# Layer 1's last group: another order for DVE's and ScalarE's steps behind the last convolution and in the closing ring

## The chip, the cores and the metric

The kernel runs on one core of one Trainium2 chip. The core has five engines that follow their own instruction lists and wait for one another on semaphores: TensorE (PE) multiplies matrices into PSUM banks, VectorE (DVE) and ScalarE (ACT) do elementwise work, GpSimd (POOL) does elementwise work and starts some transfers, and SyncE (SP) starts the others. The metric is the device time of one execution in microseconds (us), as the median of several runs.

## The reference

The computation is a two-layer decoder trunk on 512 tokens of 1024 channels, in float32. Layer 0 mixes tokens by causal pooling, layer 1 by sliding-window attention. Behind each mixer comes a gated MLP with a causal depthwise convolution of width 3, and at the end a final RMS norm:

```python
def rms_norm(x, g):
    xf = x.astype(jnp.float32)
    y = xf * lax.rsqrt(jnp.mean(xf * xf, axis=-1, keepdims=True) + RMS_EPS)
    return (y * g.astype(jnp.float32)).astype(x.dtype)

def conv_glu_ffn(h, w_in, conv_w, conv_b, w_out):
    u = h @ w_in
    c = conv(u, conv_w) + conv_b          # causal, depthwise, width 3
    a, g = c[..., :D_FF], c[..., D_FF:]
    return (a * jax.nn.silu(g)) @ w_out

def reference(x, ...):
    h = x
    for i in range(DEPTH):
        hn = rms_norm(h, norm_mix[i])
        ...
        h = h + mix
        hn = rms_norm(h, norm_ffn[i])
        h = h + conv_glu_ffn(hn, ffn_w_in[i], ffn_conv_w[i], ffn_conv_b[i], ffn_w_out[i])
    return rms_norm(h, norm_f)
```

`D_FF` is 2816. The change lies at the very end: in the last part of layer 1's `(a * silu(g)) @ w_out`, the residual add and the final norm.

## The kernel before

Every float32 product is made of three matmuls. Each operand is split into a high part, rounded by ScalarE (`A.activation(h, raw, AF.Copy)`, L105 for weights, L774 for activations), and a low part, the rest, which DVE subtracts (L108, L776). `mm3` issues high by high (L89), high by low or low by high (L90), and the third cross product (L91).

**Layer 1's MLP, first half** (`mlp_in`). The 2816 hidden channels are 22 blocks of 128, each with a gate half (s = 1) and a value half (s = 0). For each half TensorE fills a PSUM bank with the product over all 512 tokens. `conv_chunk` then makes the convolution of it: ScalarE scales the bank by the last tap (L689), DVE adds the two shifted taps (L690, L691). The gate goes through ScalarE's silu (L750), and DVE multiplies the halves (L761).

**Layer 1's MLP, second half** (`mlp_tokens`). Pairs of blocks and pairs of token halves are multiplied by Strassen's scheme with seven products instead of eight. For this DVE forms sums and differences of a block pair's activations (L765 to L767, tile `y`); `split_sum` splits them into `zh` and `zl` (L774, L776), seven slices of 256 tokens. The output weights come as blocks a11, a12, a22 and as sums s1 to s4, each split in the same way. The 11 pairs of blocks are worked in three groups of 4, 4 and 3 pairs (`GROUPS`); the change touches the last one, for which `end` is set. Its pairs come in a first set of two and a second set of one. The second set's pair is block pair 10, the last one, so its `zh` and `zl` come last of all. The steps of this group are a11 of both sets, s1, a12 and s2 of the first set, s1, a12 and s2 of the second, and then s4, s3 and a22 of both sets. Each step makes two banks (q = 0 and 1), one per token quarter of 128.

A step's banks are added into the residual tile `ht`, which holds tokens in rows. In the last group a11, s1 and s2 are subtracted at L905 in `evict`. The banks that complete half a quarter's row go to the class `Last`. `left` takes the first 512 channels of a token quarter (quarters 0 and 1 behind a12, 2 and 3 behind s4) and `right` the others (quarters 2 and 3 behind s3, 0 and 1 behind a22). Both call `gather`: DVE adds the bank (L957), ScalarE squares and sums the row (L959, tile `n_sq`, sums in `ss`). `gained` lets GpSimd multiply the left half by the norm's gain (L964, tile `hg`). The reciprocal root is made of tiny steps of one element a row: two scalings on DVE (L996, L997), a square root on ScalarE (L969, `rs_y`), then on DVE L970, a reciprocal (L971) and one Newton step (L976, L977) into `r`. `store` scales the two halves by `r`, the right one on DVE (L985) and the left one on ScalarE (L987), and sends both out (L989). This handing of a quarter from engine to engine is the ring. Before the first square, `gather` has ScalarE load its square-root table (L954, then L123), with an input from the last `zh`.

**What sets the order.** Most instructions are placed by the framework's scheduler, which lists each engine's instructions at build time. `tc.issue_after(x)` keeps an instruction behind `x`, and `pin` keeps the pinned instructions of an engine in program order. On the chip every engine works its list strictly in order. In the last group the scheduler may place all weight splits but three, and the subtractions of L905, only behind the last sum of the activations (`sums[-1]`, L767).

Two banks (76 and 77, `alpha`) are reused by a11, s2, s3 and a22 in turn, so TensorE's first matmul of s2 waits until DVE has subtracted a11's bank.

Of the kernel before, what the change touches and what calls it, by code (L numbers as in the profile page):

```python
# [23 lines left out]
ALU = mybir.AluOpType  # L24
# [3 lines left out]
D = 1024  # L28
# [9 lines left out]
NF = FF // P  # L38
# [24 lines left out]
def trunk(ctx: ExitStack, tc: tile.TileContext, x_tok, x_t, vecs, w_pool, w_kq, w_v, w_o, gain, w_in, w_half, w_down, w_tok, out):  # L63
# [630 lines left out]
    def mlp_in(fp, layer, xs, norm, z, turns):  # L694
# [25 lines left out]
        for i, group in enumerate(groups):  # L720
# [21 lines left out]
            for n, ((j, s), ps) in enumerate(zip(group, pss)):  # L742
                with ExitStack() as order:
                    for x in () if i else behind[: 3 + n // 2]:
                        order.enter_context(tc.issue_after(x.ins))
                    conv[s] = conv_chunk(fp, layer, ps, None if i else rb, s * NF + j, f"c{layer}_{j}_{s}")
                if i:
                    turn(3, *taps[-2:])
                if s == 1:
                    silu = A.activation(conv[1], conv[1], AF.Silu)  # L750
                    if i:
                        turn(1, silu, taps[-1])
                    continue
                e, odd = divmod(j, 2)
                if not odd:
                    y = fp.tile([P, 8, HS], F32, tag="y", name=f"y{layer}_{e}", bufs=1)
                    zh = fp.tile([P, 7, HS], F32R, tag="zh", name=f"zh{layer}_{e}", bufs=5)
                    zl = fp.tile([P, 7, HS], F32R, tag="zl", name=f"zl{layer}_{e}", bufs=5)
                    z.append((zh, zl))
                o = y[:, 2 * odd : 2 * odd + 2, :].rearrange("p a b -> p (a b)")  # L760
                V.tensor_tensor(o, conv[0], conv[1], ALU.mult)  # L761
                if not odd:
                    split_sum(y, z[e], 0, 0, 1, -1.0)
                else:
                    V.tensor_tensor(y[:, 4:6, :], y[:, 0:2, :], y[:, 1:4:2, :], ALU.subtract)  # L765
                    V.tensor_tensor(y[:, 6, :], y[:, 4, :], y[:, 3, :], ALU.add)
                    sums.append(V.tensor_tensor(y[:, 7, :], y[:, 2, :], y[:, 6, :], ALU.subtract))  # L767
                    split_sum(y, z[e], 2, 1, 6)
                yield j

# [9 lines left out]
    def mlp(fp, xs, norm):  # L780

        z, ht = [], []
        turns = turned(fp, ht)
        up = mlp_in(fp, 1, xs, norm, z, turns)
        done, first = 0, 0
        for g, n in enumerate(GROUPS):
            upto = first + 2 * n
            end = Last(fp, z, ht) if upto == NF else None
            while done < min(upto + 1, NF):
                done = next(up) + 1  # L790
                if end and done in (NF - 3, NF - 2):
                    end.split("a22" if done == NF - 3 else "a12", g)
            for x in turns:
                pass
            mlp_tokens(g, z[first // 2 : upto // 2], ht, end)
            first = upto

    def turned(fp, ht):
# [15 lines left out]
                    )  # L814
                    yield

    def mlp_tokens(g, z, ht, end):

        sets = [(sum(SETS[g][:i]), sum(SETS[g][: i + 1])) for i in range(len(SETS[g]))]
        raws, banks_of = {}, {}  # L820
# [44 lines left out]
        def ready(upto):  # L865
            while todo and len(ws) < upto + kept:
                x = todo.pop(0)
                with ExitStack() as order:
                    if end and x not in (("a11", 0), ("a11", 1), ("s1", 0)):
                        order.enter_context(tc.issue_after(sums[-1].ins))  # L870
                    ws[x] = split(*x)

# [33 lines left out]

        used = 0
        for kind, s in steps:
            ready(used + AHEAD + 1)
            used += not end or (kind, s) not in end.ws  # L910
            name = KINDS[kind][1]
# [16 lines left out]
    class Last:  # L928
        def __init__(self, fp, z, ht):
# [1 line left out]
            self.r = small(fp, NT, 32, name="r3", bufs=1)  # L931
            self.ss = small(fp, 2 * NT, 32, name="ss3", bufs=1)
            self.root_in = small(fp, 1, 32, name="root1_in", bufs=1)
            self.fp, self.ws = fp, {}

        def split(self, kind, g):
            whole = tuple(
# [28 lines left out]
        def root(self, t):  # L966
            v, e = self.mid[t]
            s1 = self.ss[:, 2 * t + 1 : 2 * t + 2]
            pin(A.activation(e, s1, AF.Sqrt, bias=e, scale=1.0 / D))  # L969
            pin(V.scalar_tensor_tensor(v, s1, -0.5 / D, v, ALU.mult, ALU.add))  # L970
            pin(V.reciprocal(e, e))  # L971

        def newton(self, t):
            v, e = self.mid[t]
            x = self.tiny("t")
            pin(V.scalar_tensor_tensor(x, e, e, v, ALU.mult, ALU.mult))  # L976
            pin(V.scalar_tensor_tensor(self.r[:, t : t + 1], x, 1.5, e, ALU.add, ALU.mult))  # L977

# [12 lines left out]
        def left(self, t, ps):  # L991
            self.gather(t, 0, ps)
            self.gained(t, 0)
            v, e = self.mid[t] = self.tiny("v"), self.tiny("y")
            s0 = self.ss[:, 2 * t : 2 * t + 1]
            pin(V.tensor_scalar(v, s0, -0.5 / D, -0.5 * EPS, ALU.mult, ALU.add))  # L996
            pin(V.tensor_scalar(e, s0, 1.0 / D, EPS, ALU.mult, ALU.add))  # L997

        def right(self, t, ps):
            last, was = t == 1, self.prev  # L1000
            if was is not None:
                self.root(was)
            self.gather(t, 1, ps)
            if was is not None:
                self.newton(was)
                if not last:
                    self.store(was)
            self.prev = t

        def close(self):  # L1010
            self.store(0, (1,))
            self.root(1)
            self.store(0, (0,))
            self.newton(1)
            self.store(1, eng=A)

    norm0, norm1, norm2 = (Norm(f"n{i}") for i in range(3))
    xs0, xs1, xs2 = [], [], []
# [354 lines left out]
```

## Time and profile before

| what | value |
|---|---|
| median of 3 runs | 892.71 us (892.08 to 893.31) |
| profiled execution, its own time | 892.47 us |
| span of the profiled execution | 890.4 us |
| granted TensorE clock | 0.997 |
| TensorE busy | 878.3 us, 99% of the span |
| DVE busy | 702.4 us, 79% |
| ScalarE busy | 509.3 us, 57% |
| GpSimd busy | 252.7 us, 28% |

The span runs from the first to the last instruction; the device time has 2.07 us more around it. In the rows of a timeline the columns are the start in the span, the duration, the engine, the line, the operation and its output and inputs with their shapes. At the end, in brackets, stands the idle time of the engine ahead of the instruction and what ended it. Consecutive instructions of one engine overlap a little, so the distance from start to start is what one costs its queue. The end of the kernel, from the last matmul of the convolution on, is the part from about 852 us to 890.4 us.

### The profile page before, as it was taken

How to read it: one execution, taken by the hardware profiler on the slowest of the kernel's cores; microseconds unless marked ns; L12 is line 12 of the kernel's file. 1: busy time of each engine (PE TensorE's matmuls, PEld its weight loads, DVE VectorE, ACT ScalarE, POOL GpSimd, SP SyncE). 2: the span in 40 equal slices, each digit the busy share in tenths (PEclk: the TensorE clock that was granted, in tenths of full speed). 3: DMA queues.
4: the chain of work that ended last, by engine and by line, in shares of the span. 5: the costliest groups of instructions: out<-in, count | busy, mean ns of one | idle time of the engine just before them, and what ended most of it. 6: DMA issues, size and time to landing. Idle time of an engine off the chain costs nothing.

```text
span 890.4 us, 12922 instructions
## 1 busy us (share of the span) xinstructions
PE 878.3 (99%) x4720; PEld 760.1 (85%) x4720; DVE 702.4 (79%) x1106; ACT 509.3 (57%) x851; POOL 252.7 (28%) x331
## 2 busy tenths in 40 slices
PE   8999999999999999999999999999999999999996
PEld 8888889999999998888888888888888888888875
DVE  6989998888788886765887386997876777866886
ACT  7856655646455553635888365887634444434544
POOL 4767332222213110335765040000330002200212
PEclk9999999999999999999999999999999999999998
DMA  8444346565555542222110042364486221572332
GB/s 323 143 138 119 110 135 180 148 172 148 145 155 155 127 144 81 73 95 95 49 48 25 1 144 93 112 170 144 89 209 199 95 95 48 136 231 83 119 71 95
DMA packets 38559, 109.98 MB, mean 124 GB/s; under 512 B 4064, under 2 KB 6112, under 8 KB 38496
## 3 DMA queue, kind: packets, MB, share of 16 engines
q1 hardware_dynamic: 34464, 95.26, 33.0%
q0 software_dynamic: 3888, 13.63, 9.0%
q8 instruction: 37, 0.61, 0.3%
q10 hardware_dynamic: 144, 0.26, 0.1%
q14 instruction: 26, 0.21, 0.1%
HBM read 107.04 MB, written 2.10 MB: 123 GB/s over the span
## 4 chain that ended last, share of the span: by engine, by line
PE 83%; DVE 12%; ACT 3%; issue 2%; DMA 1%; POOL 0%; ACTq 0%; DVEq 0%
PE bank L89 26%; PE bank L90 26%; PE bank L91 26%; PE bank L1208 1%; PE bank L1236 1%; DVE bank L395 1%; PE bank L290 1%; DVE tl L414 1%; PE bank L257 1%; ACT sc L1224 1%; DVE uw_hold_l L470 1%; DVE a_t L376 1%; DVE a_t L361 0%; DVE wt_a_l L108 0%; DMA wi_raw<-w_in 0%
## 5 line engine op out<-in xcount | busy, mean ns | idle before, releaser
L89 PE MATMUL bank<-f1x_h,wi_h 128*128 128x512 f32 x352 | 137.1, 389 | 0.0
L90 PE MATMUL bank<-f1x_l,wi_h 128*128 128x512 f32 x352 | 136.9, 389 | 0.0
L91 PE MATMUL bank<-f1x_h,wi_l 128*128 128x512 f32 x352 | 136.8, 389 | 0.0
L105 ACT ACTIVATE wi_h<-wi_raw 128x1024 fp32r<-128x1024 f32 x58 | 61.4, 1058 | 58.7 <-PE bank L90 38.3
L108 DVE TENSOR_TENSOR wi_l<-wi_raw,wi_h 128x1024 fp32r<-128x1024 f32 x44 | 53.8, 1222 | 37.0 <-ACT wi_h L105 36.9
L91 PEld LDWEIGHTS bank<-f1x_h,wi_l 128*128 128x128 f32 x352 | 66.1, 188 | 14.0 <-DVE wi_l L108 0.2
L89 PEld LDWEIGHTS bank<-f1x_h,wi_h 128*128 128x128 f32 x352 | 66.1, 188 | 13.7
L90 PEld LDWEIGHTS bank<-f1x_l,wi_h 128*128 128x128 f32 x352 | 66.1, 188 | 13.6
L487 POOL TENSOR_TENSOR uw_r_raw<-uw_r_raw,uw_u_raw 128x512 f32<-128x512 f32 x15 | 25.0, 1667 | 161.7 <-DVE uw_hold_l L470 148.9
L108 POOL TENSOR_TENSOR wi_l<-wi_raw,wi_h 128x256 fp32r<-128x256 f32 x56 | 53.1, 979 | 29.4 <-ACT wi_h L105 19.0
L842 POOL TENSOR_TENSOR wt_a_raw<-wt_a_raw,wt_s_raw 128x1024 f32<-128x1024 f32 (+1 forms) x6 | 13.9, 2322 | 144.4 <-DVE wt_a_l L108 141.8
L91 PE MATMUL bank<-th,uw_hold_l 128*128 128x256 f32 x180 | 50.9, 283 | 0.0
L90 PE MATMUL bank<-tl,uw_hold_h 128*128 128x256 f32 x180 | 50.9, 283 | 0.0
L89 PE MATMUL bank<-th,uw_hold_h 128*128 128x256 f32 x180 | 50.8, 282 | 0.0
L830 POOL DMA_DIRECT2D wt_s_raw<-w_tok x12 | 10.4, 869 | 141.0 <-DMA wt_s_raw<-w_tok 86.3
L222 POOL TENSOR_TENSOR n_acc<-n_acc,n_sq 128x512 f32<-128x512 f32 x13 | 19.1, 1468 | 86.6 <-ACT n_sq L213 86.5
L90 PE MATMUL bank<-f0x_l,wi_h 128*128 128x512 f32 x112 | 43.6, 389 | 0.0
L91 PE MATMUL bank<-f0x_h,wi_l 128*128 128x512 f32 x112 | 43.6, 389 | 0.0
L89 PE MATMUL bank<-f0x_h,wi_h 128*128 128x512 f32 x112 | 43.0, 390 | 0.0
L469 ACT ACTIVATE uw_hold_h<-wo_raw 128x512 fp32r<-128x512 f32 (+1 forms) x48 | 28.4, 591 | 25.4 <-PE bank L90 18.8
L533 DVE TENSOR_TENSOR h<-bank,h 128x512 f32<-128x512 f32 x48 | 32.9, 686 | 11.9 <-PE bank L91 11.4
L689 ACT ACTIVATE c_t<-bank,vec 128x512 f32<-128x512 f32 x44 | 33.4, 766 | 8.2 <-PE bank L91 5.2
(440 smaller groups left out, 2826.7 us busy)
## 6 DMA issues: line engine op xcount, KB each, us to landing
wi_raw<-w_in SPq DMA_DIRECT2D x58, 512.0 KB, 3.3
wo_raw<-w_down SPq DMA_DIRECT2D x32, 256.0 KB, 2.7
uw_u_raw<-w_half SPq DMA_DIRECT2D x15, 512.0 KB, 5.6
uw_u_raw<-w_half POOLq DMA_DIRECT2D x15, 512.0 KB, 5.7
uw_r_raw<-w_half SPq DMA_DIRECT2D x15, 512.0 KB, 3.5
wt_a_raw<-w_tok SPq DMA_DIRECT2D x15, 512.0 KB, 3.9
wt_s_raw<-w_tok SPq DMA_DIRECT2D x11, 512.0 KB, 3.9
kq_raw<-w_kq SPq DMA_DIRECT2D x10, 512.0 KB, 3.3
```

The lines of the kernel that those rows point to most:

```text
L89: T.matmul(ps, lhsT=wh, rhs=xh, start=start, stop=False, **kw)
L90: T.matmul(ps, lhsT=wh, rhs=xl, start=False, stop=False, **kw)
L91: T.matmul(ps, lhsT=wl, rhs=xh, start=False, stop=stop, **kw)
L105: pin(A.activation(h[:, :n], raw[:, :n], AF.Copy))
L108: lows.append((eng or V).tensor_tensor(l[:, o], raw[:, o], h[:, o].bitcast(F32), ALU.subtract))
L222: eng.tensor_tensor(self.acc[:, lo:hi], self.acc[:, lo:hi], sq[:, lo:hi], ALU.add)
L469: A.activation(w[0], raw, AF.Copy)
L487: G.tensor_tensor(r[:, :n], r[:, :n], u[:, n:], ALU.add)
L533: V.tensor_tensor(h[m], ps, h[m], ALU.add)
L689: taps.append(A.activation(t, ps, AF.Identity, bias=col(V_CB + layer * 2 * NF + m), scale=cw[2]))
L830: pin(G.dma_start(r[:, :n], src[:, b1, :], accum_op=ALU.add))
L842: G.tensor_tensor(r[:, :n], r[:, :n], raws["s1", s][:, :n], ALU.add)
```

## The change

The diff:

```diff
--- before.py
+++ after.py
@@ -765,6 +765,8 @@
                     V.tensor_tensor(y[:, 4:6, :], y[:, 0:2, :], y[:, 1:4:2, :], ALU.subtract)
                     V.tensor_tensor(y[:, 6, :], y[:, 4, :], y[:, 3, :], ALU.add)
                     sums.append(V.tensor_tensor(y[:, 7, :], y[:, 2, :], y[:, 6, :], ALU.subtract))
+                    if j == NF - 1:
+                        yield j
                     split_sum(y, z[e], 2, 1, 6)
                 yield j
 
@@ -792,7 +794,7 @@
                     end.split("a22" if done == NF - 3 else "a12", g)
             for x in turns:
                 pass
-            mlp_tokens(g, z[first // 2 : upto // 2], ht, end)
+            mlp_tokens(g, z[first // 2 : upto // 2], ht, end, up)
             first = upto
 
     def turned(fp, ht):
@@ -814,7 +816,7 @@
                     )
                     yield
 
-    def mlp_tokens(g, z, ht, end):
+    def mlp_tokens(g, z, ht, end, up):
 
         sets = [(sum(SETS[g][:i]), sum(SETS[g][: i + 1])) for i in range(len(SETS[g]))]
         raws, banks_of = {}, {}
@@ -867,6 +869,7 @@
                 x = todo.pop(0)
                 with ExitStack() as order:
                     if end and x not in (("a11", 0), ("a11", 1), ("s1", 0)):
+                        order.enter_context(tc.issue_after(taps[-2].ins))
                         order.enter_context(tc.issue_after(sums[-1].ins))
                     ws[x] = split(*x)
 
@@ -906,6 +909,8 @@
 
         used = 0
         for kind, s in steps:
+            if end and (kind, s) == ("a12", 0):
+                next(up)
             ready(used + AHEAD + 1)
             used += not end or (kind, s) not in end.ws
             name = KINDS[kind][1]
@@ -931,7 +936,7 @@
             self.r = small(fp, NT, 32, name="r3", bufs=1)
             self.ss = small(fp, 2 * NT, 32, name="ss3", bufs=1)
             self.root_in = small(fp, 1, 32, name="root1_in", bufs=1)
-            self.fp, self.ws = fp, {}
+            self.fp, self.ws, self.due = fp, {}, []
 
         def split(self, kind, g):
             whole = tuple(
@@ -967,12 +972,13 @@
             v, e = self.mid[t]
             s1 = self.ss[:, 2 * t + 1 : 2 * t + 2]
             pin(A.activation(e, s1, AF.Sqrt, bias=e, scale=1.0 / D))
-            pin(V.scalar_tensor_tensor(v, s1, -0.5 / D, v, ALU.mult, ALU.add))
-            pin(V.reciprocal(e, e))
 
         def newton(self, t):
             v, e = self.mid[t]
             x = self.tiny("t")
+            s1 = self.ss[:, 2 * t + 1 : 2 * t + 2]
+            pin(V.scalar_tensor_tensor(v, s1, -0.5 / D, v, ALU.mult, ALU.add))
+            pin(V.reciprocal(e, e))
             pin(V.scalar_tensor_tensor(x, e, e, v, ALU.mult, ALU.mult))
             pin(V.scalar_tensor_tensor(self.r[:, t : t + 1], x, 1.5, e, ALU.add, ALU.mult))
 
@@ -991,28 +997,31 @@
         def left(self, t, ps):
             self.gather(t, 0, ps)
             self.gained(t, 0)
+            self.halves()
+            self.due.append(t)
+
+        def halves(self):
+            while self.due:
+                self.half(self.due.pop())
+
+        def half(self, t):
             v, e = self.mid[t] = self.tiny("v"), self.tiny("y")
             s0 = self.ss[:, 2 * t : 2 * t + 1]
             pin(V.tensor_scalar(v, s0, -0.5 / D, -0.5 * EPS, ALU.mult, ALU.add))
             pin(V.tensor_scalar(e, s0, 1.0 / D, EPS, ALU.mult, ALU.add))
 
         def right(self, t, ps):
-            last, was = t == 1, self.prev
-            if was is not None:
-                self.root(was)
+            was, self.prev = self.prev, t
             self.gather(t, 1, ps)
+            self.halves()
+            self.root(t)
             if was is not None:
                 self.newton(was)
-                if not last:
-                    self.store(was)
-            self.prev = t
+                self.store(was, (1, 0))
 
         def close(self):
-            self.store(0, (1,))
-            self.root(1)
-            self.store(0, (0,))
-            self.newton(1)
-            self.store(1, eng=A)
+            self.newton(self.prev)
+            self.store(self.prev, eng=A)
 
     norm0, norm1, norm2 = (Norm(f"n{i}") for i in range(3))
     xs0, xs1, xs2 = [], [], []
```

It has three parts. First, the generator `mlp_in` stops ahead of the last `split_sum` and is resumed by `mlp_tokens` ahead of a12's first step; `ready` also keeps most weight splits behind the second last tap (`taps[-2]`, ScalarE's first step of the last convolution). On DVE the steps behind the last convolution then stand in another order. In these lists `y` is the tile of the last block pair's sums, `wt_0` and `wt_1` are the weights of the first and second set, banks 76 and 77 hold a11's two quarters; before:

```order
L767 TENSOR_TENSOR y_10_7875<-y_10_7875 128x256
L108 TENSOR_TENSOR wt_0_s_l<-wt_0_a_raw,wt_0_s_h 128x1024
L905 TENSOR_TENSOR ht<-ht,bank_76 128x512
L776 TENSOR_TENSOR zl_10_7877<-y_10_7875,zh_10_7876 128x1536
L905 TENSOR_TENSOR ht<-ht,bank_77 128x512
L108 TENSOR_TENSOR wt_1_s_l<-wt_1_s_raw,wt_1_s_h 128x512
L108 TENSOR_TENSOR wt_1_s_l<-wt_1_a_raw,wt_1_s_h 128x512
L108 TENSOR_TENSOR wt_0_s_l<-wt_0_s_raw,wt_0_s_h 128x1024
```

now:

```order
L767 TENSOR_TENSOR y_10_7875<-y_10_7875 128x256
L108 TENSOR_TENSOR wt_0_s_l<-wt_0_a_raw,wt_0_s_h 128x1024
L908 TENSOR_TENSOR ht<-ht,bank_76 128x512
L908 TENSOR_TENSOR ht<-ht,bank_77 128x512
L108 TENSOR_TENSOR wt_1_s_l<-wt_1_s_raw,wt_1_s_h 128x512
L778 TENSOR_TENSOR zl_10_7877<-y_10_7875,zh_10_7876 128x1536
L108 TENSOR_TENSOR wt_1_s_l<-wt_1_a_raw,wt_1_s_h 128x512
L108 TENSOR_TENSOR wt_0_s_l<-wt_0_s_raw,wt_0_s_h 128x1024
```

The subtraction from bank 77 stands next to that from bank 76, and the `zl` of the last pair has moved behind it and behind the low part of the second set's s1 weights.

On ScalarE, from the silu of the last block's gate (`c_21_1_t`) on, before:

```order
L750 ACTIVATE c_21_1_t<-c_21_1_t 128x512
L105 ACTIVATE wt_0_s_h<-wt_0_a_raw 128x1024
L689 ACTIVATE c_21_0_t<-bank_72,vec 128x512
L105 ACTIVATE wt_1_s_h<-wt_1_s_raw 128x512
L105 ACTIVATE wt_1_s_h<-wt_1_a_raw 128x512
L774 ACTIVATE zh_10_7876<-y_10_7875 128x1536
L105 ACTIVATE wt_0_s_h<-wt_0_s_raw 128x1024
L954 ACTIVATE root_in<-zh_10_7876 128x1
L123 ACT_TABLE_LOAD
L123 ACTIVATE root_8074<-root_in 128x1
```

now:

```order
L750 ACTIVATE c_21_1_t<-c_21_1_t 128x512
L689 ACTIVATE c_21_0_t<-bank_72,vec 128x512
L105 ACTIVATE wt_0_s_h<-wt_0_a_raw 128x1024
L105 ACTIVATE wt_1_s_h<-wt_1_s_raw 128x512
L105 ACTIVATE wt_1_s_h<-wt_1_a_raw 128x512
L776 ACTIVATE zh_10_7876<-y_10_7875 128x1536
L959 ACTIVATE root_in<-zh_10_7876 128x1
L123 ACT_TABLE_LOAD
L123 ACTIVATE root_8074<-root_in 128x1
L105 ACTIVATE wt_0_s_h<-wt_0_s_raw 128x1024
L105 ACTIVATE wt_1_s_h<-wt_1_s_raw 128x512
```

The last convolution's first step, from bank 72, stands ahead of the high part of the first set's s2 weights (`wt_0_a_raw`), and the table load with its two neighbours stands ahead of the high part of s4's weights.

Second, as a consequence of the moved program text, the low parts of s3's weights stand behind both left adds of a12 and both subtractions of s2 on DVE.

Third, in `Last`, the two scalings that follow a left add are kept in a list (`due`) and issued behind the next add; the square root of a quarter is issued straight behind its right add and its sum of squares; the two DVE steps ahead of the Newton step move from `root` to `newton`, so they follow the next quarter's add; and a quarter's store, its right half first, is issued for each quarter behind the next one's add. On DVE the last two turns of the ring were, before (`rs_v`, `rs_y`, `rs_t` and `r` are the tiny steps, `o` the stores):

```order
L957 TENSOR_TENSOR ht<-ht,bank_76 128x512
L976 SCALAR_TENSOR_TENSOR rs_t<-rs_y,rs_v 128x1
L977 SCALAR_TENSOR_TENSOR r_7552<-rs_t,rs_y 128x1
L985 SCALAR_TENSOR_TENSOR o_8206<-ht,r_7552,gainb 128x512
L970 SCALAR_TENSOR_TENSOR rs_v<-ss_7553,rs_v 128x1
L971 RECIPROCAL rs_y<-rs_y 128x1
L957 TENSOR_TENSOR ht<-ht,bank_77 128x512
L976 SCALAR_TENSOR_TENSOR rs_t<-rs_y,rs_v 128x1
L977 SCALAR_TENSOR_TENSOR r_7552<-rs_t,rs_y 128x1
L985 SCALAR_TENSOR_TENSOR o_8227<-ht,r_7552,gainb 128x512
L970 SCALAR_TENSOR_TENSOR rs_v<-ss_7553,rs_v 128x1
L971 RECIPROCAL rs_y<-rs_y 128x1
```

now:

```order
L962 TENSOR_TENSOR ht<-ht,bank_76 128x512
L980 SCALAR_TENSOR_TENSOR rs_v<-ss_7553,rs_v 128x1
L981 RECIPROCAL rs_y<-rs_y 128x1
L982 SCALAR_TENSOR_TENSOR rs_t<-rs_y,rs_v 128x1
L983 SCALAR_TENSOR_TENSOR r_7552<-rs_t,rs_y 128x1
L991 SCALAR_TENSOR_TENSOR o_8204<-ht,r_7552,gainb 128x512
L962 TENSOR_TENSOR ht<-ht,bank_77 128x512
L980 SCALAR_TENSOR_TENSOR rs_v<-ss_7553,rs_v 128x1
L981 RECIPROCAL rs_y<-rs_y 128x1
L982 SCALAR_TENSOR_TENSOR rs_t<-rs_y,rs_v 128x1
L983 SCALAR_TENSOR_TENSOR r_7552<-rs_t,rs_y 128x1
L991 SCALAR_TENSOR_TENSOR o_8228<-ht,r_7552,gainb 128x512
```

An add no longer stands between a reciprocal and its Newton step; all the tiny steps and the store of a quarter stand together behind the next quarter's add.

## The prediction

> **What bounds the kernel now.** I read the page's head and the granted clock first, to see which engine sets the time.
>
> ```profile
> span 890.4 us, 12922 instructions
> ...
> PE 878.3 (99%) x4720; PEld 760.1 (85%) x4720; DVE 702.4 (79%) x1106; ACT 509.3 (57%) x851; POOL 252.7 (28%) x331
> ```
>
> ```profile
> core 0: 890.4 us, clock 0.997
> ```
>
> TensorE is busy for 99% of the span at a full clock, so an edit in the order of DVE and ScalarE is worth what TensorE waits for them, plus what runs after its last matmul. The instructions on every engine are the same ones up to the last convolution's end, so only the last 40 us can move. Next, the timeline of TensorE there.
>
> ```profile
> 861.40 0.39 PE L91 MATMUL bank<-wt_a_zh,zl 128*128 128x512 f32 x1
> 861.98 0.47 PE L89 MATMUL bank<-wt_s_h,zh 128*128 128x512 f32 x1 [0.18 <-DVE ht L905]
> ...
> 863.19 0.39 PE L91 MATMUL bank<-wt_s_h,zl 128*128 128x512 f32 x1
> 864.15 0.50 PE L89 MATMUL bank<-wt_s_h,zh 128*128 128x512 f32 x1 [0.57 <-DVE ht L905]
> ...
> 868.38 0.39 PE L89 MATMUL bank<-wt_s_h,zh 128*128 128x512 f32 x1
> ...
> 881.76 0.39 PE L91 MATMUL bank<-wt_a_zh,zl 128*128 128x512 f32 x1
> ```
>
> Behind 861.40 the program has 84 matmuls: s2 of the first set (12), s1, a12 and s2 of the second (6 each), s4, s3 and a22 (18 each). From 868.38 to 881.76 are 59 steps in 13.38 us, 0.2268 us a step. 84 steps would take 19.05 us; they took 20.36. **1.31 us** are lost, all at the two rows that wait for DVE's subtraction at L905 (0.58 and 0.96 instead of 0.23, and a slow start behind each).
>
> Why that subtraction is late shows in the timelines of DVE and ScalarE.
>
> ```profile
> 856.19 0.75 DVE L690 SCALAR_TENSOR_TENSOR c_t<-bank,vec,c_t 128x511 f32<-128x511 f32 x1 [2.37 <-ACT c_t L689]
> ...
> 859.67 0.42 DVE L767 TENSOR_TENSOR y<-y 128x256 f32<-128x256 f32 x1
> 860.01 1.22 DVE L108 TENSOR_TENSOR wt_s_l<-wt_a_raw,wt_s_h 128x1024 fp32r<-128x1024 f32 x1
> 861.15 0.68 DVE L905 TENSOR_TENSOR ht<-ht,bank 128x512 f32<-128x512 f32 x1
> 861.75 1.75 DVE L776 TENSOR_TENSOR zl<-y,zh 128x1536 fp32r<-128x1536 f32 x1
> 863.41 0.68 DVE L905 TENSOR_TENSOR ht<-ht,bank 128x512 f32<-128x512 f32 x1
> 864.01 0.69 DVE L108 TENSOR_TENSOR wt_s_l<-wt_s_raw,wt_s_h 128x512 fp32r<-128x512 f32 x1
> ```
>
> ```profile
> 853.91 0.63 ACT L750 ACTIVATE c_t<-c_t 128x512 f32<-128x512 f32 x1 [2.13 <-DVE c_t L691]
> 854.45 1.04 ACT L105 ACTIVATE wt_s_h<-wt_a_raw 128x1024 fp32r<-128x1024 f32 x1
> 855.40 0.76 ACT L689 ACTIVATE c_t<-bank,vec 128x512 f32<-128x512 f32 x1
> ...
> 860.13 1.49 ACT L774 ACTIVATE zh<-y 128x1536 fp32r<-128x1536 f32 x1 [2.93 <-DVE y L767]
> ...
> 862.67 1.28 ACT L123 ACT_TABLE_LOAD   x1
> ```
>
> DVE runs without a gap from 856.19 on. The weights' high part at 854.45 holds back the last convolution's first step by 0.95 us (854.45 to 855.40); the long `zl` stands between the two subtractions.
>
> Last the ring, by DVE's and then ScalarE's rows of the last two turns.
>
> ```profile
> 881.98 0.75 DVE L985 SCALAR_TENSOR_TENSOR o<-ht,r,gainb 128x512 f32<-128x512 f32 x1
> 882.64 0.15 DVE L970 SCALAR_TENSOR_TENSOR rs_v<-ss,rs_v 128x1 f32<-128x1 f32 x1
> 883.20 0.16 DVE L971 RECIPROCAL rs_y<-rs_y 128x1 f32<-128x1 f32 x1 [0.41 <-ACT rs_y L969]
> 883.28 0.67 DVE L957 TENSOR_TENSOR ht<-ht,bank 128x512 f32<-128x512 f32 x1
> 883.87 0.21 DVE L976 SCALAR_TENSOR_TENSOR rs_t<-rs_y,rs_v 128x1 f32<-128x1 f32 x1
> ...
> 884.31 0.75 DVE L985 SCALAR_TENSOR_TENSOR o<-ht,r,gainb 128x512 f32<-128x512 f32 x1
> 884.98 0.15 DVE L970 SCALAR_TENSOR_TENSOR rs_v<-ss,rs_v 128x1 f32<-128x1 f32 x1
> 885.07 0.16 DVE L971 RECIPROCAL rs_y<-rs_y 128x1 f32<-128x1 f32 x1
> ...
> 885.72 0.75 DVE L985 SCALAR_TENSOR_TENSOR o<-ht,r,gainb 128x512 f32<-128x512 f32 x1
> ```
>
> ```profile
> 882.28 0.71 ACT L987 ACTIVATE o<-hg,r 128x512 f32<-128x512 f32 x1
> 882.89 0.28 ACT L969 ACTIVATE rs_y<-ss,rs_y 128x1 f32<-128x1 f32 x1
> ...
> 884.74 0.29 ACT L969 ACTIVATE rs_y<-ss,rs_y 128x1 f32<-128x1 f32 x1
> ```
>
> The last matmul ends at 881.76 + 0.39 = 882.15, but DVE adds its bank only at 883.28: **1.13 us** late. In front of that add stands the reciprocal of the turn before, which waits for a square root, which ScalarE does only behind a store's scaling (882.28, then 882.89). The ring turns in 2.33 us (881.98 to 884.31), and TensorE delivers a bank every 9 x 0.2268 = 2.04.
>
> **The change, part by part.** No instruction is added or removed.
>
> *ScalarE, the convolution's step ahead of the high part.* It can start at 854.45, 0.95 us earlier, and DVE's chain to `y` L767 goes with it: 858.72 instead of 859.67. Could the bank be late? The silu at 853.91 already waits for DVE's work on the other half's bank; the last bank's matmuls come before the weights `wt_a` on TensorE, and the row at 855.40 waits for nothing. Gain for the chain 0.95; if the silu sits later it would be less, at worst 0. I take 0.95. The high part ends some 0.6 us later (about 856.15) and is read by DVE at 859.06: covered.
>
> *DVE, both subtractions ahead of `zl`.* Low part 859.06, first subtraction 860.20, second 860.80 (0.60 behind, as 861.15 to 861.75), done 861.48. An unhindered TensorE wants the banks at 861.40 + 0.23 = 861.63 and six steps later, 862.99. Both stalls go: **-1.31 us**. If only the order counted and the chain stayed, the second would be done at 862.43, still in time, and the first would still cost its 0.35 and its slow start: the lower end is about -0.85.
>
> *What is late next.* `zl` now stands behind the second subtraction and one low part (0.60 + 0.61): it runs 862.0 to 863.76. Its reader, the third matmul of s1's second set, is step 15: 861.40 + 3.40 = 864.80. Margin 1.0 us; from there each us of delay is a us of stall. The table load goes ahead of s4's high part on ScalarE: `zh` at 859.18, the load's 1.28 and its two small neighbours end near 862.3, the high part near 863.3, its low part on DVE near 865.5, while s4 is step 31, 868.43. Covered by 2.9 us.
>
> *s3's low parts go behind both left adds and the s2 evictions.* The rows that decide:
>
> ```profile
> 868.96 1.22 DVE L108 TENSOR_TENSOR wt_s_l<-wt_s_raw,wt_s_h 128x1024 fp32r<-128x1024 f32 x1
> ...
> 872.13 1.01 DVE L108 TENSOR_TENSOR wt_s_l<-wt_s_raw,wt_s_h 128x512 fp32r<-128x512 f32 x1
> ```
>
> ```profile
> 869.13 3.46 POOL L964 TENSOR_TENSOR hg<-ht,gainb 128x512 f32<-128x512 f32 x2 [3.80 <-DVE ht L957]
> ```
>
> s2's last matmul is step 30, done at 868.6; with a half step in front of it, its eviction starts near 869.15 and s3's low part near 869.75, done 870.97. It is read at step 50, 872.74; the second set's low part follows within 0.7 us and is read at step 56, 874.10. Margin 1.8 us alone. GpSimd's two products fall on the same stretch: with both ahead, from the first left add's end (863.7 + low parts of 0.60, 1.14 and 0.60 + three bank reads: 867.9) for the 3.46 us of the row, the low parts begin at 871.4 and end at 872.6 and 873.2. That is still in time, by 0.1 us. I take 0.
>
> The 512-wide low part at 872.13 took 1.01 us beside GpSimd's products, and 0.69 at 864.01 without them. [...]
>
> *The ring.* The square root of a turn now follows its own sum of squares, a turn ahead of its reciprocal, and the add of a bank waits only for TensorE and for the store before it. A turn on DVE is then add 0.59 (883.28 to 883.87), first small step 0.09 (884.98 to 885.07), reciprocal to store 0.65 (885.07 to 885.72), store 0.67 (884.31 to 884.98): 2.00 us, under TensorE's 2.04. So the last add starts at the last matmul's end and not 1.13 behind it; I leave 0.03 for the hand-over, as between 855.40 + 0.76 and 856.19. **-1.10 us**. The bounds: all of it, or, should a turn take over 2.04 (each 0.1 us over costs some 0.2 by the last), about -0.8.
>
> *Behind the last add* two turns' small steps and stores now follow one another: 0.59 + 0.09 + 0.65 + 0.67 + 0.09 + 0.65 = 2.74 us to the last store's start, where before it was 885.72 - 883.28 = 2.44. **+0.30 us**. The last square root ends 1.75 us behind the add (885.03 - 883.28) and is wanted 2.09 behind it: covered. From the last store's start to the end of the span (890.4 - 885.72 = 4.68 us) nothing changes: the same transfers, and again two of them at the very end.
>
> *Sum*: -1.31 - 1.10 + 0.30 = **-2.11 us**. The profiled execution took 892.47 (2.07 around its span): 890.36. The median, 892.71, lies 0.24 above it: 890.60. I forecast **890.6**, 0.24% faster.
>
> **The rivals.**
>
> *A new wait takes the stall's place* (chance 0.20). `zl` with 1.0 us of margin, or s3's low parts with 0.1 to 1.8, stop TensorE. If they eat the whole 1.31, the last add is at 882.18, the last store at 884.92 instead of 885.72: 0.8 gained, **891.9**. [...]
>
> *The end is hidden anyway* (0.08). If what follows the last store (4.68 us) depends on the stores ahead and not on the last one, an earlier ring changes nothing: **892.7**. Against it: the last store's row is also the last of the two engines' work, and in the new ring the earlier stores start as much earlier as the last.
>
> *Slower: the second set's s3 weights come late* (0.05). Their first half is fetched by SyncE once s2's low part is done, 0.95 us earlier than now, so further into the first set's accumulating transfer; GpSimd adds the second half once it has landed.
>
> ```profile
> L829 SPq DMA_DIRECT2D wt_s_raw<-w_tok x12: 327/328/328, 576.1 to 861.3; - x12
> ```
>
> ```profile
> 864.47 0.86 POOL L830 DMA_DIRECT2D wt_s_raw<-w_tok  x1 [6.72 <-ACT root L123]
> ...
> DMA to landing us min/median/max: 3.7/7.1/10.3
> ```
>
> ```profile
> DMA to landing us min/median/max: 2.6/3.9/6.9
> ```
>
> Issued at 861.3, followed by GpSimd at 864.47, the first landing took about 2.6, the least of its line. From 860.4, with the longest landings (6.9, 0.5 to GpSimd, 10.3), the weights are there at 878.1, their low part 1.2 us later (0.5 of ScalarE, 0.69 of DVE), against 874.1: 5.2 us of stall, 3.1 slower than now, **895.8**. It costs anything only above 12.0 us of landings together, and outweighs the gain above 14.1. Today's two are near 6.3 by the least of both lines.
>
> **How the numbers follow.** Forecast 0.67, rivals 0.20, 0.08 and 0.05. The forecast's own range is 890.0 to 891.2 (half a microsecond of the runs' spread, 892.08 to 893.31, on either side); with the first rival and half of the second it is 889.8 to 892.2. A measurement of this kernel tells about 0.2%, 1.8 us, from no change: 890.9. Of the forecast's 0.67 some 0.56 lie below that, and 0.02 of the first rival: faster 0.58, same 0.37, slower 0.05.
>
> **What would show it.** Right: 84 matmuls behind the last a12 step of the first set in about 19.1 us, with no row waiting for the evictions; the last add within 0.1 us of the last matmul's end; 2.7 us from it to the last store; no wait of the reciprocal for ScalarE. Wrong: a matmul that waits for `zl` or for s3's low part, a ring that turns in more than 2.04 us, or the last store earlier by 2 us and the span's end not.

## The result and the profile after

The changed kernel takes **889.59 us** (median of 7 runs, 889.28 to 890.89) against 892.71 us (892.08 to 893.40, 7 runs): ratio 0.9967, 95% interval 0.9955 to 0.9978. It is faster by 0.33%, where 0.24% was forecast, and the median lies 0.2 us below the range of the forecast (889.8 to 892.2). The head of its page and its clock:

```profile
span 888.1 us, 12923 instructions
...
PE 877.7 (99%) x4720; PEld 760.4 (86%) x4720; DVE 702.3 (79%) x1106; ACT 509.2 (57%) x851; POOL 252.3 (28%) x331
```

```profile
core 0: 888.1 us, clock 0.998
```

The busy times are those of before within 0.6 us; the span is 2.3 us shorter. Where it went shows in TensorE's timeline, at the places of the two old waits and at the end:

```profile
861.26 0.39 PE L91 MATMUL bank<-wt_a_zh,zl 128*128 128x512 f32 x1
861.49 0.39 PE L89 MATMUL bank<-wt_s_h,zh 128*128 128x512 f32 x1
...
862.62 0.39 PE L91 MATMUL bank<-wt_s_h,zl 128*128 128x512 f32 x1
862.85 0.39 PE L89 MATMUL bank<-wt_s_h,zh 128*128 128x512 f32 x1
...
864.66 0.39 PE L91 MATMUL bank<-wt_s_h,zl 128*128 128x512 f32 x1
...
880.30 0.39 PE L91 MATMUL bank<-wt_a_zh,zl 128*128 128x512 f32 x1
```

Both steps are 0.23 us now. The 84 matmuls behind 861.26 take 880.30 - 861.26 = 19.04 us, as many as 84 steps of 0.2267. The matmul at 864.66 is the first reader of the last `zl`. DVE, from the last sum on:

```profile
858.72 0.42 DVE L767 TENSOR_TENSOR y<-y 128x256 f32<-128x256 f32 x1
859.06 1.22 DVE L108 TENSOR_TENSOR wt_s_l<-wt_a_raw,wt_s_h 128x1024 fp32r<-128x1024 f32 x1
860.19 1.28 DVE L908 TENSOR_TENSOR ht<-ht,bank 128x512 f32<-128x512 f32 x2
861.39 0.69 DVE L108 TENSOR_TENSOR wt_s_l<-wt_s_raw,wt_s_h 128x512 fp32r<-128x512 f32 x1
861.99 1.75 DVE L778 TENSOR_TENSOR zl<-y,zh 128x1536 fp32r<-128x1536 f32 x1
...
864.26 1.82 DVE L108 TENSOR_TENSOR wt_s_l<-wt_s_raw,wt_s_h 128x1024 fp32r<-128x1024 f32 x2
...
869.71 2.50 DVE L108 TENSOR_TENSOR wt_s_l<-wt_s_raw,wt_s_h 128x1024 fp32r<-128x1024 f32 x2
...
880.00 0.75 DVE L991 SCALAR_TENSOR_TENSOR o<-ht,r,gainb 128x512 f32<-128x512 f32 x1
880.73 0.69 DVE L962 TENSOR_TENSOR ht<-ht,bank 128x512 f32<-128x512 f32 x1
881.33 0.15 DVE L980 SCALAR_TENSOR_TENSOR rs_v<-ss,rs_v 128x1 f32<-128x1 f32 x1
881.40 0.16 DVE L981 RECIPROCAL rs_y<-rs_y 128x1 f32<-128x1 f32 x1
...
882.04 0.75 DVE L991 SCALAR_TENSOR_TENSOR o<-ht,r,gainb 128x512 f32<-128x512 f32 x1
...
883.42 0.75 DVE L991 SCALAR_TENSOR_TENSOR o<-ht,r,gainb 128x512 f32<-128x512 f32 x1
```

The chain stands within 0.02 us of where the prediction's walk through the rows put it: the last sum at 858.72, the subtractions from 860.19, `zl` complete at 863.74, 0.92 us ahead of its reader. The last add starts at 880.73, 0.04 behind the last matmul's end (880.30 + 0.39); the reciprocal waits for nothing. The ring turns with TensorE, in 2.04 us (880.00 to 882.04). From the last add to the last store are 2.69 us. Two rows of each trace are needed for what follows: the first `zh` of the last block pair on ScalarE, and TensorE's first matmul of a11 of the first set. In the kernel before and then in the changed one they are:

```profile
849.75 0.42 ACT L774 ACTIVATE zh<-y 128x256 fp32r<-128x256 f32 x1 [6.64 <-DVE y L761]
...
852.11 0.39 PE L89 MATMUL bank<-wt_a_h,zh 128*128 128x512 f32 x1
```

```profile
849.74 0.42 ACT L776 ACTIVATE zh<-y 128x256 fp32r<-128x256 f32 x1 [6.65 <-DVE y L761]
...
851.97 0.39 PE L89 MATMUL bank<-wt_a_h,zh 128*128 128x512 f32 x1
```

The `zh` comes 2.36 us ahead of the matmul in the trace of before and 2.23 us in this one. Step by step the walk holds on the side of DVE, ScalarE and the ring. What it lacks is this distance and the numbers around the walk.

### The profile page after: what moved, and what is told of

It is laid out like the page before. It is cut to its first block, busy times and chain, and to the rows that moved or that the text cites. A ratio compares the mean times of both kernels' runs of the same rounds, so it can differ in the third digit from the quotient of the medians.

```text
span 888.1 us, 12923 instructions
## 1 busy us (share of the span) xinstructions
PE 877.7 (99%) x4720; PEld 760.4 (86%) x4720; DVE 702.3 (79%) x1106; ACT 509.2 (57%) x851; POOL 252.3 (28%) x331
## 4 chain that ended last, share of the span: by engine, by line
PE 89%; DVE 9%; issue 1%; ACT 1%; POOL 0%; DVEq 0%; ACTq 0%
PE bank L89 28%; PE bank L90 28%; PE bank L91 28%; PE bank L1217 1%; PE bank L1245 1%; DVE bank L395 1%; PE bank L290 1%; DVE tl L414 1%; PE bank L257 1%; DVE uw_hold_l L470 1%; DVE a_t L376 1%; ACT sc L1233 0%; DVE a_t L361 0%; DVE g_t L360 0%; DVE ty L422 0%
```

## The experiments

Five lengths are read from every trace below. The *stage* runs from the `zh` with 256 columns, the first one of the last pair, to the end of the span: 849.75 to 890.41, 40.66 us, in before, and 849.74 to 888.13, 38.39, in the changed kernel. The *distance* is the time from this `zh` to the first matmul of a11 of the first set (2.36 and 2.23). The *84 steps* are TensorE's behind a12 of the first set (20.36 and 19.04). The *lag* is the time from the last matmul's end to the last add (1.13 and 0.04). The *time around the span* is the device time less the span; it is given over all executions of a kernel, whose spans are on record to 0.1 us.

| kernel | device time: median, mean (runs) | around the span | stage | distance | 84 steps | lag | last add to last store |
|---|---|---|---|---|---|---|---|
| before, profiled before the change | 892.71, 892.72 (7) | 2.07 in the profile | 40.66 | 2.36 | 20.36 | 1.13 | 2.44 |
| before again | 892.37, 892.63 (11) | 2.02 to 2.11 | 40.61 | 2.17 | 20.50 | 1.14 | 2.43 |
| before, lines shifted | 892.02, 892.10 (8) | 2.03 to 2.11 | 40.64 | 2.10 | 20.57 | 1.14 | 2.43 |
| changed | 889.59, 889.74 (7) | 1.78 to 1.86 | 38.39 | 2.23 | 19.04 | 0.04 | 2.69 |
| changed, second time | 889.68, 889.83 (6) | 1.81 to 1.88 | 38.39 | 2.24 | 19.04 | 0.04 | 2.69 |
| changed, third time | 889.39, 889.79 (7) | 1.78 to 1.89 | 38.37 | 2.22 | 19.04 | 0.03 | 2.69 |
| convolution's end alone | 890.66, 890.79 (8) | 1.66 to 1.75 | 39.21 | 2.07 | 19.03 | 1.30 | 2.43 |
| ring alone | 890.92, 891.13 (11) | 1.67 to 1.73 | 39.78 | 2.22 | 20.45 | 0.04 | 2.69 |
| DVE's order alone | 891.39, 891.40 (11) | 1.67 to 1.75 | 40.15 | 2.99 | 19.04 | 1.31 | 2.44 |
| DVE's order alone, second time | 891.58, 891.66 (8) | 1.66 to 1.76 | 40.16 | 2.46 | 19.41 | 1.48 | 2.43 |
| ScalarE's order alone | 891.11, 891.16 (11) | 2.01 to 2.12 | 39.69 | 2.02 | 19.72 | 1.14 | 2.43 |
| changed, `zl` twice | 891.28, 891.28 (8) | 2.03 to 2.12 | 39.93 | 2.20 | 20.62 | 0.03 | 2.70 |

### The changed kernel again, and before against itself

Both without an edit. In the expectations below, the walk is the prediction's step-by-step reckoning through the rows.

> The changed kernel once more, unaltered, to see whether the 0.8 us by which it beat the walk is of the kernel or of the few executions measured. By the walk (stalls -1.31, ring -1.10, longer end +0.30) it is 2.1 us below the kernel before; with the spans of the two profiled executions 2.3. If the extra gain belongs to the kernel it is again 2.9 to 3.1 us below.

Measured: 889.68 us against 892.32 (25 runs), ratio 0.9965, interval 0.9953 to 0.9977. The extra gain did not go away with a second set of executions, and the stage is 38.39 us to the hundredth.

> The kernel before against itself, to see how much a median of this many runs moves by itself, and how far its span and the time around its span differ from execution to execution. Ratio 1.000, the medians within 0.5 us of each other; the span 890 to 891 with 1.8 to 2.1 us around it. If the profiled execution of before was a low one, the typical span is above 890.4 and the gain of the change is more than its two traces show.

Measured: ratio 0.9998 (0.9989 to 1.0007), medians 892.37 and 892.32. The span of before went from 889.7 to 892.0 over the 25 executions, so the profiled 890.4 was an ordinary one. The time around the span was 2.02 to 2.11 in all of them; in the changed kernel it was 1.78 to 1.88. The prediction had carried before's 2.07 over. That is some 0.2 us of the gain it missed.

### The two parts apart

Convolution's end alone: the first part of the diff, with the class `Last` of before.

```diff
+                    if j == NF - 1:
+                        yield j
                     split_sum(y, z[e], 2, 1, 6)
...
+                        order.enter_context(tc.issue_after(taps[-2].ins))
                         order.enter_context(tc.issue_after(sums[-1].ins))
...
+            if end and (kind, s) == ("a12", 0):
+                next(up)
             ready(used + AHEAD + 1)
```

> Only the first part: the order behind the last convolution on DVE and ScalarE; the ring as before. By the walk TensorE's two waits at the evictions go and nothing else: 1.3 us below the kernel before, the last add still about 1.1 us behind the last matmul and 2.4 us from it to the last store. If the extra gain sits in this part: 2.1 below. If the old ring gives the time back (it turns in 2.33 us and not with TensorE): less than 0.5 below.

Ring alone: the class `Last` of the changed kernel in the kernel before.

```diff
         def right(self, t, ps):
-            last, was = t == 1, self.prev
-            if was is not None:
-                self.root(was)
+            was, self.prev = self.prev, t
             self.gather(t, 1, ps)
+            self.halves()
+            self.root(t)
             if was is not None:
                 self.newton(was)
-                if not last:
-                    self.store(was)
-            self.prev = t
+                self.store(was, (1, 0))
```

(with `half`, `halves`, `root`, `newton` and `close` as in the change)

> Only the ring: adds, small steps, roots and stores in the new order, with the convolution's end as before. By the walk TensorE still loses 1.3 us at its two waits, the last add starts with the last matmul's end and the end behind it is 0.3 longer: 0.8 us below the kernel before. If the extra gain sits in this part: 1.6 below. If s3's low parts, which move with the ring, stop TensorE: a wait at s3's first products and no gain.

Measured: 0.9977 (0.9967 to 0.9987) and 0.9983 (0.9974 to 0.9992). The stage is 1.43 us shorter with the convolution's end (40.64, the mean of the three traces of before, less 39.21) and 0.86 with the ring (less 39.78); together 2.29, and the whole change gives 2.25. The waits and the ring's lag were expected to give 1.3 and 0.8. The parts add up to some hundredths, so no gain of another kind larger than the scatter of the distances (0.1 to 0.2 us) is left in the stage. By their means the device times are 1.86 and 1.52 us below before's (892.64), 0.43 and 0.66 more than the stages; 0.36 us of each is the time around the span, 1.70 in both builds against 2.06.

DVE's rows of the convolution's end alone show what the old ring does behind a TensorE that no longer waits:

```profile
881.29 0.75 DVE L990 SCALAR_TENSOR_TENSOR o<-ht,r,gainb 128x512 f32<-128x512 f32 x1
881.96 0.15 DVE L975 SCALAR_TENSOR_TENSOR rs_v<-ss,rs_v 128x1 f32<-128x1 f32 x1
882.52 0.16 DVE L976 RECIPROCAL rs_y<-rs_y 128x1 f32<-128x1 f32 x1 [0.41 <-ACT rs_y L974]
882.60 0.67 DVE L962 TENSOR_TENSOR ht<-ht,bank 128x512 f32<-128x512 f32 x1
883.18 0.21 DVE L981 SCALAR_TENSOR_TENSOR rs_t<-rs_y,rs_v 128x1 f32<-128x1 f32 x1
883.43 0.16 DVE L982 SCALAR_TENSOR_TENSOR r<-rs_t,rs_y 128x1 f32<-128x1 f32 x1
883.63 0.75 DVE L990 SCALAR_TENSOR_TENSOR o<-ht,r,gainb 128x512 f32<-128x512 f32 x1
```

It still turns in 2.34 us with the 0.41 us wait for the root, and the last add (882.60) is 1.30 behind the last matmul's end instead of 1.13: it gives 0.17 us back. Behind the last convolution no row of DVE waits for TensorE in this trace, where in the kernel before one add did:

```profile
873.35 0.69 DVE L957 TENSOR_TENSOR ht<-ht,bank 128x512 f32<-128x512 f32 x1 [0.20 <-PE bank L91]
```

So the end comes here from DVE's and ScalarE's own chain, and the 1.43 us say how much shorter that chain became, not only what TensorE gained.

In the ring alone TensorE keeps both waits, and the first is longer than in the trace of before:

```profile
860.73 0.39 PE L91 MATMUL bank<-wt_a_zh,zl 128*128 128x512 f32 x1
861.43 0.47 PE L89 MATMUL bank<-wt_s_h,zh 128*128 128x512 f32 x1 [0.32 <-DVE ht L905]
...
862.67 0.40 PE L91 MATMUL bank<-wt_s_h,zl 128*128 128x512 f32 x1
863.61 0.51 PE L89 MATMUL bank<-wt_s_h,zh 128*128 128x512 f32 x1 [0.54 <-DVE ht L905]
```

The first step is 0.70 us here, against 0.58 in the trace on which the prediction rests, the second 0.94 against 0.96, and 84 steps are 20.45 instead of 20.36. The end of the wait is set by DVE, its beginning by TensorE, and how far the two are apart differs from execution to execution: the distance is 2.02 to 2.46 us in eleven of the twelve traces and 2.99 in one.

### The two halves of the convolution's end

DVE's order alone: the stop ahead of the last `split_sum` and its resumption, without `issue_after(taps[-2].ins)`. ScalarE's order alone: that line, without the stop.

> Only DVE's order behind the last convolution (the second subtraction and one low part ahead of zl); ScalarE's order and the ring as before. By the walk the second wait of TensorE goes and the first stays at 0.35 to 0.5 us with its slow start of 0.1: 0.9 to 1.0 us of stall gone from the last stage, 0.9 us below the kernel before on the trace. If DVE's chain has to come forward for any gain: less than 0.3.

> Only ScalarE's order behind the last convolution (the convolution's first step ahead of the weights' high part, the table load ahead of s4's high part); DVE's order and the ring as before. By the walk DVE's chain comes 0.95 us forward, the first subtraction is in time and the second ends near 863.1, some 0.1 us late with a slow start: 1.2 to 1.3 us of stall gone. If zl between the two subtractions is the whole cause: about 0.4 gone.

Measured: 0.9991 (0.9982 to 1.0000) and 0.9987 (0.9978 to 0.9996); stages 0.49 and 0.95 us shorter, where 0.9 and 1.2 to 1.3 were expected. Together 1.44, the 1.43 of both. The waits came out otherwise than expected. With DVE's order TensorE found every bank ready; in that execution the last pair's first `zh` stood 2.99 us ahead of the stage's first matmul and not 2.1 to 2.4. With ScalarE's order the second wait was longer than the 0.1 us expected:

```profile
860.32 0.68 DVE L906 TENSOR_TENSOR ht<-ht,bank 128x512 f32<-128x512 f32 x1
860.91 1.75 DVE L776 TENSOR_TENSOR zl<-y,zh 128x1536 fp32r<-128x1536 f32 x1
862.58 0.68 DVE L906 TENSOR_TENSOR ht<-ht,bank 128x512 f32<-128x512 f32 x1
```

```profile
862.54 0.39 PE L91 MATMUL bank<-wt_s_h,zl 128*128 128x512 f32 x1
863.32 0.50 PE L89 MATMUL bank<-wt_s_h,zh 128*128 128x512 f32 x1 [0.39 <-DVE ht L906]
```

DVE is where the walk had it (862.58 against 862.46), but TensorE wants the bank at 862.77 and not at 862.99: here too it is earlier against DVE than in the first trace, and the expected 1.2 to 1.3 us became 0.8 of the 84 steps (19.72 against 20.48, the mean of before's three traces). DVE's order was profiled once more, since its first execution had an unusual distance:

> DVE's new order alone, a second look, since in the first one DVE and ScalarE happened to be some 0.7 us ahead of their usual place against TensorE, and TensorE found every bank ready. With DVE at its usual place (first zh of the last pair some 2.1 to 2.4 us ahead of the stage's first matmul) the first wait is there, 0.35 to 0.6 us with 0.1 of slow start, the second is not: the 84 matmuls take 19.5 to 19.8 us. If the order alone removes both waits, 19.05 again.

Measured: 84 steps in 19.41 us, somewhat under the expected 19.5 to 19.8; the first step 0.48 instead of 0.23 with 0.07 of slow start behind it, the second wait gone. So DVE's order alone removes the second wait and leaves the first at an ordinary distance, which bears out that the 2.99 us were why it was missing the first time. The stage is the same in both executions (40.15 and 40.16), although TensorE's last matmul ended 31.71 us behind the first `zh` in one and 31.55 in the other. The last add, first time and second, shows why:

```profile
881.90 0.67 DVE L961 TENSOR_TENSOR ht<-ht,bank 128x512 f32<-128x512 f32 x1
```

```profile
882.34 0.67 DVE L961 TENSOR_TENSOR ht<-ht,bank 128x512 f32<-128x512 f32 x1
```

It comes 33.02 and 33.03 us behind the first `zh` (848.88 and 849.31). With the old ring and this order no row of DVE behind the last convolution waits for TensorE, so the end follows DVE's and ScalarE's chain, and the lag takes up what TensorE does (1.31 and 1.48). The 0.49 us are what the new order takes off that chain, as the 0.95 of ScalarE's order are what the earlier convolution step takes off it; that is why the two add up. The ratio the second time is 0.9995 (0.9984 to 1.0006), not to be told from no change.

### How much room `zl` had

The changed kernel with `zl` of the last pair subtracted twice:

```diff
                     split_sum(y, z[e], 2, 1, 6)
+                    if j == NF - 1:
+                        again(y, z[e], 2, 1, 6)
...
+    def again(y, z, i, o, n):
+        src = y[:, i : i + n, :].rearrange("p a b -> p (a b)")
+        h, l = (t[:, o : o + n, :].rearrange("p a b -> p (a b)") for t in z)
+        V.tensor_tensor(l, src, h.bitcast(F32), ALU.subtract)
```

> The changed kernel with the 1536 wide subtraction of zl made twice on DVE, the second time behind s2's low part, so that zl is complete 2.27 us later (0.60 and 1.67). This measures how much room zl had. By the margin of the walk (0.9 to 1.0 us) TensorE waits once, at the first matmul of s1's second set that reads zl, 1.3 to 1.5 us, and the end comes as much later. If there was no room, 2.3 us; if zl's reader does not matter, 0.

TensorE's rows at the first reader of `zl`, and DVE's of the two subtractions:

```profile
864.04 0.39 PE L90 MATMUL bank<-wt_s_l,zh 128*128 128x512 f32 x1
865.70 0.50 PE L91 MATMUL bank<-wt_s_h,zl 128*128 128x512 f32 x1 [1.27 <-DVE zl L778]
```

```profile
861.62 1.75 DVE L785 TENSOR_TENSOR zl<-y,zh 128x1536 fp32r<-128x1536 f32 x1
...
863.89 1.75 DVE L778 TENSOR_TENSOR zl<-y,zh 128x1536 fp32r<-128x1536 f32 x1
```

TensorE waits there and nowhere else: a step of 1.66 instead of 0.23, with 0.1 of slow start. The stage is 1.54 us longer than the changed kernel's; the ratio to before is 0.9989 (0.9979 to 0.9999). `zl` was 2.27 us later, so 0.8 to 0.9 us of it were room, as the walk said (0.9 to 1.0). This also shows the first rival's mechanism at work, at a delay that the change itself doesn't have.

### The time around the span, and a third time

Before with nine empty lines ahead of it.

> The kernel before with nine empty lines ahead of it: the same instructions with other line numbers. Looks at the time around the span, which was 2.02 to 2.11 us in every execution of before and 1.78 to 1.88 in every one of the changed kernel. If it hangs on the order of the instructions or on nothing in the text: 2.06 again. If it hangs on how the program is laid out as a file: another value, constant over its executions. Span as before.

Measured: 2.03 to 2.11 us around the span, and the stage of before (40.64); ratio 0.9998 (0.9987 to 1.0008). Line numbers do not matter.

> The changed kernel a third time, to see what is left once the stage of the change is known. By the traces the stage from the last pair's first zh to the end is 2.25 us shorter (40.61 to 40.66 against 38.39), and the time around the span 0.24 us (2.06 against 1.82): 2.5 us below the kernel before, ratio 0.9972. The 2.8 to 3.0 of the first two comparisons would then hold 0.3 to 0.5 of the part that both kernels share, whose length differs from execution to execution. If those belong to the change, it is 2.9 or more again, and the time ahead of that first zh is shorter too.

Measured: 889.39 against 892.70 (11 runs), ratio 0.9970 (0.9959 to 0.9982), the stage 38.37. Over all comparisons before took 892.42 on the mean (104 executions, the shifted copy among them) and the changed kernel 889.78 (20): 2.64 us. The stage is 2.25 of it and the time around the span 0.23. Left are 0.16 us, with a standard error of 0.14 from the scatter of the executions (0.64 and 0.54 us): no gain ahead of the stage is shown.

## Why the prediction was wrong in size

Its mechanism and the signs of all its terms stood: TensorE's two waits went, no new one came, the ring closed up with TensorE, the end behind the last add grew. The sizes fell short: 2.11 us were reckoned, 2.64 measured over all comparisons and 3.12 in the first one. The time fell outside the range for these reasons.

1. **"The profiled execution took 892.47 (2.07 around its span): 890.36."** This is a step that failed: 2.07 us were carried over to a kernel that has 1.78 to 1.89. On the means (2.06 and 1.83) that is 0.23 us.
2. **"The median, 892.71, lies 0.24 above it: 890.60."** This step failed too: it took the gap between one execution and the median of three others for a property of the kernel and handed it on. Before takes 892.42 on the mean of 104 executions, so its profiled one was ordinary and its median high; in the changed kernel the profiled execution took 889.96, and the median lies 0.37 below it. Without either one of these two steps the forecast is 0.24 us lower, and the same range would just have held the median.
3. **"-1.31 us"** for the waits was mis-sized: it is what one execution lost, in which TensorE came 0.1 to 0.3 us later than in the others. The distance was 2.36 us in that trace and 2.10 to 2.24 in the other traces of before and in the changed kernel's. Before lost 1.46 and 1.53 us in the two other traces (20.50 and 20.57 against 19.04), the ring alone 1.41. The changed kernel's TensorE runs through, so its stage counts from TensorE's place: the measured 2.25 us at 2.23 of distance would be 2.12 at the 2.36 of the first trace, the 2.11 of the sum. The walk from DVE's side, whose rows set the end of the wait, was right to 0.02 us.
4. **"-1.10"** and **"+0.30"** measured -1.09 (1.13 to 0.04) and +0.25 (2.44 to 2.69). The turn of 2.00 us stayed under TensorE's 2.04, as reckoned.
5. **The range's lower end**, 889.8, lay 0.8 us below the forecast. It came from half the spread of three runs of before, and the last 0.2 of it from no rival, since every rival is slower than the forecast. The waits' size and the time around the span were both taken as known, with no bounds of their own on the side of a larger gain. Medians of before alone went from 892.09 to 892.71 us over its comparisons (7 to 33 executions each). Of the 1.01 us between forecast and median 0.53 are the gain's, and 0.48 are the scatter of the two medians of this comparison against the means (0.29 and 0.19).

The first rival, a new wait, did not come: `zl` had 0.92 us of room and s3's low parts about 1.0. The rows at 869.71 and 864.26 show two subtractions of the same shapes: they take 2.50 us beside GpSimd's products and 1.82 without them. GpSimd's pair ends at 870.52, 0.81 us behind the start of the first subtraction, and 0.68 us are added. What adds them no run shows.

```profile
867.96 2.56 POOL L969 TENSOR_TENSOR hg<-ht,gainb 128x512 f32<-128x512 f32 x2 [2.90 <-DVE ht L962]
```

The pair itself took 2.56 us, not 3.46. Before, it started beside a low part of DVE's (868.96, 1.22 us), now beside adds from PSUM, with the low parts only from 869.71 on; whether that alone makes the 0.90 us is not shown. The bound with 0.1 us of room was not reached. The second rival, an end that does not follow, is out: from the last store's start to the span's end are 4.7 us in every trace. The third, late weights, is out for these executions: the first half was issued at 860.35 instead of 861.32 and took longer to land, 3.3 us instead of 2.6, so that GpSimd followed at 864.20 and not 864.47, 0.27 us earlier instead of 0.9; TensorE waited for nothing behind it. One thing was put down to the wrong part ahead of the result: s3's low parts move with the ring's new order, as the ring alone shows (both behind s2's subtractions, 870.32), and not with the first part (between the left adds as before, 868.58).

## What to carry to other kernels

A walk through the rows of the waiting engines can be right to hundredths and still miss by a fifth of the gain (2.11 of 2.64 us): size a wait from the side that ends it, allow some tenths for the side that begins it, and give the part of the device time that no row shows a range of its own. Do not carry the gap between one execution and the median of a few others over into a forecast. When a chain of engines hands work round in a ring, compare its turn with the rate at which the bound engine delivers: what lies above that rate comes back at the end (here 1.13 us of lag, with a turn of 2.33 against 2.04), and a gain made ahead of a ring that is too slow is partly eaten by it (here 0.17 us). Take parts of a change apart by a length of the trace that starts at the same instruction, since device times of builds differ by things outside the change (here by 0.36 us around the span); and look which engine sets the end of that length, since it can hide what another one gained.

## What the runs showed that was not expected

**The time around the span belongs to the build.** It was 2.01 to 2.13 us in before, in its shifted copy, in ScalarE's order alone and in the kernel with `zl` twice; 1.66 to 1.76 in the convolution's end, the ring and DVE's order alone; 1.78 to 1.89 in the changed kernel, three times. The 0.1 us within a build are no more than the rounding of the spans on record: in the profiled executions, whose spans are known to hundredths, it is 2.05 or 2.06 in the first group, 1.70 to 1.72 in the second and 1.83 to 1.85 in the third. What sets it is open: it does not follow the line numbers, nor one part of the change, nor the number of instructions in the trace (12922 in before and in the convolution's end). A difference of 0.36 us between builds is 0.04% here, and it made DVE's order alone look 0.83 us faster (891.40 against 892.23, the means of the executions taken side by side), where its stage is 0.49 shorter.

**The part that all these kernels share differs by up to 1.6 us.** The first `zh` of the last pair came between 848.88 and 850.51 us. One share is the start: the 24 warming matmuls ahead of the first products end at different times, in before and in the ring alone:

```profile
2.23 6.05 PE L257 MATMUL bank<-warm 128*128 128x144 f32 x24 [2.23 <-DVE warm L255]
```

```profile
2.23 5.17 PE L257 MATMUL bank<-warm 128*128 128x144 f32 x24 [2.23 <-DVE warm L255]
```

From start to start such a matmul costs 0.240 us at first and 0.123 once the granted clock is 1.0; the trace's clock record puts that at 6.26 us into the span in the ring alone and at 8.07 in before, where all 24 are slow. Over the twelve traces it comes between 6.15 and 8.07 us, 1.9 us apart; what sets the moment is not shown. Another share is layer 0. In the profiled execution of the convolution's end TensorE waits once more there, and longer a second time than in the other traces (0.57 to 0.66 us):

```profile
111.25 0.39 PE L89 MATMUL bank<-th,uw_u_h 128*128 128x256 f32 x1 [0.57 <-ACT sn L650]
119.56 0.50 PE L89 MATMUL bank<-z0h,uw_hold_h 128*128 128x512 f32 x1 [0.97 <-DVE h L533]
```

ScalarE's stretch from its first `uw_u_h` (weights of layer 0) to its first `kq_h` (layer 1) is 228.29 us there, against 227.11 to 227.15 in the other traces. Whether this wait is what makes some executions of before take 893 us and more is not shown.
